# A two-block network on one core: layer 0's modulation dealt out in quarters of the contraction, the attention's scaling on two engines, and products that nobody reads in the last expert

## The chip, the core and the metric

The kernel runs on one core of a Trainium2 chip, which has its own TensorE (matrix products), VectorE (DVE), ScalarE (ACT), GpSimd (POOL), SyncE (SP, which here only issues transfers) and 16 DMA engines. The metric is the device time of one launch in microseconds (us). Lower is better.

## The reference

The model is two blocks on 256 tokens of width 1024. The first block is attention of two kinds and a mixture of experts; the second has two layers with adaptive modulation, of which each needs six vectors from a small conditioning vector:

```python
# first block
h = rms_norm(x, norm1_g);  proj = h @ w_in                      # 1024 -> 3072
oa = diff_attention(qa, ka, va, lam, ...)                       # 4 heads
oa = rms_norm(oa, subln_g) * (1 - lambda_init)
od = dilated_attention(qd, kd, vd, bias_b)                      # 8 heads
x = x + concat([oa, od]) @ w_out
x = x + expert_choice_ffn(rms_norm(x, norm2_g), ...)            # 16 experts take their 32 best tokens each
x = rms_norm(x, norm_f_g)
# second block, layer i of 2, on x and on a context of 256 tokens
mod   = silu(c)     @ ada_w[i] + ada_b[i]                       # 1024 -> 6144: shift, scale, gate, twice
mod_c = silu(c_ctx) @ ada_w[i] + ada_b[i]
h = x * (1 + sc1) + sh1;  y = mixer(h, ...)                     # MLA in layer 0, a windowed attention in layer 1
x = layer_norm(alpha * x + g1 * y, ln1_g[i], ln1_b[i])
x = layer_norm(alpha * x + g2 * mlp(x * (1 + sc2) + sh2), ln2_g[i], ln2_b[i])
```

All inputs are float32, and each weight is read once.

## The kernel before, in words

The program is one stream for each engine in a fixed order, written out by hand; a tile framework adds the waits. It has three parts.

**The front** (function `front`) computes the first block up to the router. After the first three projections, a loop over n runs 16 attention units (`units`: eight of the differential kind, then eight dilated) in a pipeline: unit n makes its scores (`sc`, L652), unit n-2 is turned (`dt`, L675) and multiplied with the values (`dpv`, L683 and L700). Between the two, a table (`fill`) says at which n one of the nine remaining projections runs (`prj`, 48 products of a split into high and low halves, L176 to L178), and a second one (`ADA_PULLS`) how many steps of layer 0's modulation are pulled. Such a step (`ada`) takes two tiles of 1 MB of `ada_w` (`adaw`, four buffers), multiplies them with the conditioning vectors into four strips of 32 partitions (`adap`, L476), copies the result to `adam`, and a step later adds the strips up by four narrow products (`adac`, L446), one step for each twelfth of the 6144 columns. At n = 15 the first 512 columns of the output `o` are scaled on DVE (L763); at the end `turn_o` transposes `o` (`trp`) for the output projection (`pyf`). Two of that projection's weights are converted on ACT and POOL at the n in `WOUT_AT`. The router then picks tokens with eight-at-a-time maxima on DVE (L845, L846), after a copy of the scores out of PSUM (L842).

**The experts** (`experts`) stream 16 experts' weights through a few buffers: gate and up (`wg`, products `egg` and `egu`, L970) and down (`wd`, `ey`, L1017). The context's layer 0 runs in between.

**The tail** (`tail`) adds the last expert's result (`esc`, L1849), normalises, and runs the second block on x. A list of steps (`filler`, pulled by `pull(fill)`) computes layer 1's modulation in the background of layer 0: the first half on TensorE, the second half on DVE (L497, L499, eight steps for a chunk, then `adac`). In layer 0's MLP another list, `rest`, applies the layer norm's gain and shift to x on POOL in eight steps (L1953).

SP issues nearly all loads in program order; a load waits for its buffer, and those behind it wait with it. POOL issues layer 1's `adaw` loads and some others in its own order.

Of the kernel before, what the change touches and what calls it, by code (L numbers as in the profile page):

```python
# [9 lines left out]
F32 = mybir.dt.float32  # L10
F32R = mybir.dt.float32r
AF = mybir.ActivationFunctionType
OP = mybir.AluOpType
# [6 lines left out]
NE = 16  # L20
CAP = 32
# [8 lines left out]
COLS = {}  # L30
# [71 lines left out]

ADA_PULLS = (0, 1, 0, 1, 0, 1, 0, 1, 0, 1, 0, 1, 1, 1, 1, 1, 1, 1)
MLA_PULLS = (3, 9, 13, 16)
PROJ_PULLS = (0, 0, 1, 0, 0, 0, 0)
ADA_VECTOR = 6
WOUT_AT = (15, 16)

UNITS = 11, 4, 8 * 11 + 11 * 4
CTX_FROM = 5 * 11
# [39 lines left out]
def pull(gen, n=1):  # L152
    for _ in range(n):
        next(gen, None)


def drain(gen):
    for _ in gen:
        pass


class Kernel:
# [24 lines left out]
    def bank(self, tag, shape, name):  # L187

        return self.psp.tile(shape, F32, name=name, tag=tag, bufs=2)

    def pair(self, name):

# [226 lines left out]
    def ada(self, layer, pool, nbuf, loader, q, q2, vector=12):  # L419
# [84 lines left out]
        yield 12  # L504
        gate_rows()

    def modulation(self, name, layer, kinds, who, g=None, b=None):

        nc = self.nc
        mod = (self.mod0, self.mod1)[layer]  # L510
        sh = mod[:, kinds[0] * 8:kinds[0] * 8 + 8, who]
        sc = mod[:, kinds[1] * 8:kinds[1] * 8 + 8, who]
        t = self.cm[name]

        def col(n):
            return self.cols[:, COLS[n][0]:COLS[n][0] + 8]
        if g is None:
            nc.vector.tensor_copy(t[:, 0], sc)
        else:
            nc.vector.tensor_mul(t[:, 0], sc, col(g))  # L520
        if b is None:
            nc.vector.tensor_copy(t[:, 1], sh)
        else:
            nc.vector.tensor_mul(t[:, 1], sc, col(b))
            nc.vector.tensor_add(t[:, 1], t[:, 1], sh)


    def front(self, es, right):
        tc, nc, a = self.tc, self.nc, self.a
        q = nc.gpsimd  # L530
# [22 lines left out]
        fe = ExitStack()  # L553
        fa = self.pool(fe, "fa")
        la = Loader({"a": 4})
        ag = self.ada(0, fa, 4, la, nc.sync, nc.gpsimd)
        next(ag)


# [21 lines left out]
        for k in range(0, 8, 2):  # L581
            p = trp[k // 2].rearrange("p (a b) -> p a b", a=2)
# [27 lines left out]
        n2, _ = COLS["norm2"]  # L610
# [30 lines left out]
        o = self.s8([128, 2, D], "o")  # L641
# [62 lines left out]
        g = proj(0)  # L704
# [18 lines left out]

        drain(g2)
        drain(proj(4))
        fill = {0: 1, 1: 3, 2: 5, 4: 6, 5: 8, 6: 10, 8: 7, 9: 9, 10: 11}
        units = [("diff", h, qt) for h in range(4) for qt in range(2)]
        units += [("dil", i, qt) for i in range(4) for qt in range(2)]
        or_ = f1.tile([128, 2, 4], F32, name="or_")
        oT = [fwl.tile([128, 8, 256], F32R, name="oT" + n, tag="hT" + n) for n in "hl"]  # L730

        def turn_o(k):
            p = self.transpose_to(o, k, 2, "d", "trp2")
            self.put(oT, (slice(None), slice(k, k + 2)), p, self.col("subln", 0) if k < 4 else None)
        pend = []
        for n in range(len(units) + 2):
            if n == WOUT_AT[0]:
                self.set_slots(own + [lambda nm: self.s8([128, 2048], nm, F32R) for i in range(2)])
            if n in WOUT_AT:
                self.convert(nc.gpsimd)  # L740
            if n < len(units):
                kind, i, qt = units[n]
                pend.append((kind, i, qt, (diff_a if kind == "diff" else dil_a)(i, qt)))
            done = pend.pop(0) if n >= 2 else None
            if done:
                kind, i, qt, e = done
                pt = turn(e, 1 if kind == "diff" else 2, "dt")
            g = proj(fill[n]) if n in fill else iter(())
            next(g, None)
            pull(ag, ADA_PULLS[n])  # L750
            if done:
                (diff_b if kind == "diff" else dil_b)(i, qt, pt)
                if qt == 1:
                    for h in ((i,) if kind == "diff" else (4 + 2 * i, 5 + 2 * i)):
                        if h + NB < 12:
                            load_bias(h + NB, q)
            drain(g)
            if n == 15:
                self.rstd(or_, ossq, 1.0 / 128, 1e-5)
                for t in range(2):  # L760
                    for h in range(4):
                        oo = o[:, t, h * 128:h * 128 + 128]
                        nc.vector.tensor_scalar(oo, oo, or_[:, t, h:h + 1], 1.0 - lam_init, op0=OP.mult, op1=OP.mult)  # L763
            if n >= 16:
                turn_o(2 * (n - 16))
        turn_o(4)
        turn_o(6)
        drain(ag)

# [48 lines left out]
        p = self.bank("d", [128, 2, NE], "rl")  # L818
# [19 lines left out]
        p = self.bank("d", [128, 256], "affT")  # L838
        for tt in range(2):
            nc.tensor.transpose(p[:NE, tt * 128:tt * 128 + 128], aff[:, tt], self.ident)  # L840
        wk = f1.tile([NE, 256], F32, name="wk", tag="hot")
        nc.vector.tensor_copy(wk, p[:NE])  # L842
        m8 = f1.tile([NE, 8], F32, name="m8")
        for _ in range(CAP // 8):
            nc.vector.max(m8, wk)  # L845
            nc.vector.match_replace(wk, m8, wk, -1.0)  # L846
        nc.vector.tensor_scalar(wk, wk, 0.0, None, op0=OP.is_lt)

        sw = f1.tile([NE, 256], F32, name="slotw", tag="addt")
# [77 lines left out]
    def experts(self, es, right, xs, oh, slots):  # L927
        tc, nc, a = self.tc, self.nc, self.a
# [27 lines left out]
        for e in range(NE):  # L956
# [3 lines left out]
            for k in range(8):  # L960
# [4 lines left out]
                for n in ("w_gate", "w_up"):  # L965
                    w = le.take((n, e, k))
# [44 lines left out]
            for n in range(11):  # L1011
                w = le.take(("d", e, n))
                for h in range(2):
                    for u in range(2):
                        r, q = (2 * (n // 2) + u, n % 2) if n < 10 else (10, u)
                        s = 2 * u + (h + n) % 2
                        nc.tensor.matmul(py[h][32 * s:32 * s + 32, :], hT[:, r, q], w[:, u, h * 512:h * 512 + 512],  # L1017
                                         start=n < 2, stop=n >= 9, skip_group_check=True)
                le.done(("d", e, n))
                if le.next == len(le.items) and self.lw.hold:  # L1020

                    self.lw.hold = None
                    self.lw.pump()
                context(UNITS[2] * e + 8 * UNITS[0] + UNITS[1] * (n + 1))
# [804 lines left out]
    def tail(self, es, sg, ye, py, jk):  # L1829
# [21 lines left out]
        with ExitStack() as e1:  # L1851
# [9 lines left out]
            def square(tt, h):  # L1861
                nc.scalar.activation(jk, x[:, tt, h * 512:h * 512 + 512], AF.Square, accum_out=st[:, tt, h:h + 1])
# [14 lines left out]
            hT = self.fm(8, True, "f", "hT")  # L1877
            self.convert(nc.gpsimd, nc.vector.tensor_copy)
            self.ahead = False
            drain(self.modulate_x(hT, x, "x0a", 0))  # L1880
            square(1, 1)
            norm(1)
            kT, v = self.s8([128, 8, 256], "kTx"), self.s8([128, 2, D], "vx")
# [8 lines left out]
            n = -1  # L1892
# [72 lines left out]
        with ExitStack() as e1:  # L1965
# [5 lines left out]
            for _ in self.mlp(0, 0, hT, True, acc, lambda *t: bt.done(*t), 1):  # L1971
                n += 1
                if n >= 4:
                    pull(fill)
                    pull(rest)
                if n == 16:
                    bt = Between(rows(0, 1, "ln2_g"), "x1a", "f")
            drain(fill)
            e0.close()
# [153 lines left out]
```

## Time and profile before

| | |
|---|---|
| time, median of 3 runs | 2386.43 us (2385.85 to 2392.71) |
| the profiled execution | 2387.11 us, its span 2385.3 us |
| TensorE busy | 85% of the span, granted clock 0.899 of full speed |
| VectorE, ScalarE, GpSimd busy | 34%, 23%, 11% |
| HBM read | 783.23 MB, 329 GB/s over the span |

The span begins with the first instruction and ends with the last; the 1.8 us between it and the execution's time lie around it. Full speed of TensorE's clock is 2.4 GHz, and 0.50 is 1.2 GHz. "Share" of the DMA engines is their mean busy share.

### The profile page before, as it was taken

To read this page: it belongs to the slowest core of one execution; us is meant where nothing else is said; L and a number is where in the kernel's file an instruction comes from. 1 tells how busy PE (TensorE), PEld (TensorE's weight loads), DVE (VectorE), ACT (ScalarE), POOL (GpSimd) and SP (SyncE) were. 2 spreads that over 40 slices of the span, in tenths; PEclk is the share of its full clock that TensorE was granted. 3 is DMA by queue.
4 is the path that set the end of the run, shared out by engine and by line. 5 is a ranking of instruction groups with operands and counts; after the bars stand their busy time and mean duration, and the time that the engine had idled before them with its cause. 6 is when DMAs were issued, how large, how long until landed. Compare 5 with 4: busy or idle time off the path is not lost.

```text
span 2385.3 us, 32056 instructions
## 1 busy us (share of the span) xinstructions
PE 2019.9 (85%) x13644; PEld 1250.3 (52%) x13644; DVE 811.1 (34%) x1484; ACT 551.8 (23%) x992; POOL 255.0 (11%) x274
## 2 busy tenths in 40 slices
PE   8998778887868777877888778777999999999998
PEld 7854223442214333333333333224888999987997
DVE  5653111121211111111111111304557765377655
ACT  5432010120000000000000000004444454276443
POOL 2121000000010000000000000003213012233101
PEclk9998888899968987888888788768998999999999
DMA  9788999999999999999999999998537864334652
GB/s 336 264 329 360 421 416 418 421 410 422 416 414 420 415 400 419 417 402 419 417 417 418 389 419 409 422 422 314 208 133 245 290 218 143 97 105 147 207 177 89
DMA packets 179223, 787.60 MB, mean 330 GB/s; under 512 B 13280, under 2 KB 73928, under 8 KB 125576
## 3 DMA queue, kind: packets, MB, share of 16 engines
q1 hardware_dynamic: 154648, 694.96, 73.8%
q0 software_dynamic: 24288, 89.54, 10.2%
q8 instruction: 107, 1.75, 0.3%
q10 hardware_dynamic: 144, 1.05, 0.1%
q14 instruction: 36, 0.29, 0.0%
HBM read 783.23 MB, written 2.27 MB: 329 GB/s over the span
## 4 chain that ended last, share of the span: by engine, by line
PE 46%; DMA 40%; DVE 3%; ACT 2%; issue 1%; DVEq 0%; ACTq 0%; SPq 0%
DMA wg<-in_w_up 26%; DMA wd<-in_w_down 10%; PE ey L1017 4%; PE egu L970 4%; DMA wg<-in_w_gate 4%; PE acc L176 3%; PE acc L178 3%; PE acc L177 3%; PE ph L176 3%; PE ph L177 3%; PE ph L178 3%; PE ph L174 2%; PE py L174 2%; PE egg L970 2%; PE nqkv L176 2%; PE nqkv L177 2%
## 5 line engine op out<-in xcount | busy, mean ns | idle before, releaser
L970 PE MATMUL egu<-wg,xeT 128*32 128x352 f32 x2048 | 217.3, 551 | 114.3 <-DMA wg<-in_w_up 114.2
L381 DVE TENSOR_TENSOR wl<-cwt,wh 128x1024 fp32r<-128x1024 f32 (+1 forms) x202 | 252.8, 1294 | 59.8 <-ACT wh L380 59.6
L1017 PE MATMUL ey<-wd,hT 128*32 128x512 f32 x1408 | 207.3, 703 | 71.4 <-DMA wd<-in_w_down 71.3
L970 PE MATMUL egg<-wg,xeT 128*32 128x352 f32 x2048 | 201.2, 515 | 62.1 <-DMA wg<-in_w_gate 62.1
L380 ACT CAST wh<-cwt 128x1024 fp32r<-128x1024 f32 (+2 forms) x218 | 214.5, 1033 | 95.0 <-issue 52.3
L970 PEld LDWEIGHTS egu<-wg,xeT 128*32 128x32 f32 x2048 | 65.1, 122 | 248.2 <-DMA wg<-in_w_up 172.3
L1498 ACT ACTIVATE hu<-ph 128x512 f32<-128x512 f32 x48 | 28.7, 597 | 554.2 <-PE ph L174 447.1
L970 PEld LDWEIGHTS egg<-wg,xeT 128*32 128x32 f32 x2048 | 57.8, 116 | 187.0 <-issue 93.4
L176 PE MATMUL ph<-hTxh,wh 128*128 128x256 f32 x512 | 147.0, 287 | 1.9 <-ACT hTxh L1116 1.9
L177 PE MATMUL ph<-hTxl,wh 128*128 128x256 f32 x512 | 146.7, 286 | 0.0
L178 PE MATMUL ph<-hTxh,wl 128*128 128x256 f32 x512 | 146.4, 286 | 0.0
L1017 PEld LDWEIGHTS ey<-wd,hT 128*32 128x32 f32 x1408 | 37.6, 118 | 204.7 <-DMA wd<-in_w_down 114.4
L1519 DVE TENSOR_TENSOR accc<-accc,py 128x512 f32<-128x512 f32 x60 | 41.3, 688 | 281.3 <-PE py L174 281.3
L174 PE MATMUL py<-cwt,hs 128*128 128x512 f32 x256 | 135.6, 677 | 0.0
L174 PE MATMUL ph<-hcT,cwt 128*128 128x256 f32 x512 | 134.6, 421 | 0.0
L174 PEld LDWEIGHTS ph<-hcT,cwt 128*128 128x128 f32 x512 | 106.1, 213 | 45.3 <-issue 29.6
L1501 DVE SCALAR_TENSOR_TENSOR hs<-ph,hu 128x512 f32<-128x512 f32 x16 | 11.1, 692 | 313.4 <-ACT hu L1498 313.4
L307 POOL DMA_DIRECT2D cwt<-in_w x32 | 25.7, 803 | 806.2 <-PE ph L174 340.6
L176 PEld LDWEIGHTS ph<-hTxh,wh 128*128 128x128 f32 x512 | 99.5, 194 | 2.9 <-ACT hTxh L1116 2.4
L177 PEld LDWEIGHTS ph<-hTxl,wh 128*128 128x128 f32 x512 | 99.3, 194 | 1.0 <-issue 0.5
L178 PEld LDWEIGHTS ph<-hTxh,wl 128*128 128x128 f32 x512 | 99.4, 194 | 0.0
L176 PE MATMUL acc<-wh,hsh 128*128 128x512 f32 (+1 forms) x256 | 98.6, 385 | 0.0
(546 smaller groups left out, 3502.8 us busy)
## 6 DMA issues: line engine op xcount, KB each, us to landing
wg<-in_w_gate SPq DMA_DIRECT2D x128, 1408.0 KB, 17.8
wg<-in_w_up SPq DMA_DIRECT2D x128, 1408.0 KB, 19.1
wd<-in_w_down SPq DMA_DIRECT2D x176, 1024.0 KB, 14.2
cwt<-in_w SPq DMA_DIRECT2D x64, 1024.0 KB, 5.3
cwt<-in_w POOLq DMA_DIRECT2D x32, 1024.0 KB, 14.0
adaw<-in_ada_w SPq DMA_DIRECT2D x24, 1024.0 KB, 8.6
adaw<-in_ada_w POOLq DMA_DIRECT2D x24, 1024.0 KB, 7.8
cwt<-in_w_in SPq DMA_DIRECT2D x12, 1024.0 KB, 10.2
```

The source lines that it names most:

```text
L174: t.matmul(out, L[0], R[0], start=start, stop=stop, **kw)
L176: t.matmul(out, L[0], R[0], start=start, stop=False, **kw)
L177: t.matmul(out, L[0], R[1], start=False, stop=False, **kw)
L178: t.matmul(out, L[1], R[0], start=False, stop=stop, **kw)
L307: q.dma_start(v, src)
L380: (high or nc.scalar.copy)(parts[0][:, s], t[:, s])
L381: (eng or self.low_eng).tensor_tensor(parts[1][:, s], t[:, s], parts[0][:, s].bitcast(F32), op=OP.subtract)
L970: nc.tensor.matmul(ps[n][h][32 * j:32 * j + 32, :352], xeT[:, k, e * CAP:(e + 1) * CAP], w[:, c0:c0 + 352], start=k == 0, stop=k == 7, ski ...
L1017: nc.tensor.matmul(py[h][32 * s:32 * s + 32, :], hT[:, r, q], w[:, u, h * 512:h * 512 + 512], start=n < 2, stop=n >= 9, skip_group_check=True)
L1498: nc.scalar.activation(u, p, AF.Relu)
L1501: nc.vector.scalar_tensor_tensor(h, p, 0.0, u, op0=OP.max, op1=OP.mult)
L1519: nc.vector.tensor_add(s, s, p)
```

## The change

Six edits are made together. (1) Layer 0's modulation is written anew (`ada_wide`): a step takes two of the eight row blocks of a third of the columns, in tiles of 128 rows x 2048 columns, so each row of a transfer is 8 KB long and no longer 2 KB. Four steps add their strips in `adam` on ACT (the first) and DVE (the others), and the strips of a whole third are then added up after four transposes. (2) `fill` and `ADA_PULLS` are spread anew over n, and `WOUT_AT` is one earlier. (3) The scaling of `o` is shared by ACT and DVE, with the constant factor folded into the row factors, and `turn_o` takes the unscaled columns first. (4) The router's first maximum reads PSUM, and the copy goes. (5) In the last expert two products of 128x128 by 128x256 follow each `wd` tile; nobody reads them (`busy`). Two more pairs stand around the tail's first transposes. (6) In layer 0's MLP `rest` is pulled at every third step, and the rows for the next norm are loaded at step 36 and not at 16.

```diff
-ADA_PULLS = (0, 1, 0, 1, 0, 1, 0, 1, 0, 1, 0, 1, 1, 1, 1, 1, 1, 1)
+ADA_PULLS = (0, 1, 0, 2, 0, 0, 2, 0, 0, 2, 0, 0, 1, 0, 1, 1, 1, 1)
-WOUT_AT = (15, 16)
+WOUT_AT = (14, 15)
...
+    def busy(self, n, tag):
+        p = self.bank(tag, [128, 512], "idle")
+        z = self.sc32.rearrange("p a b -> p (a b)")
+        for i in range(n):
+            self.nc.tensor.matmul(p[:, :256], z[:, :128], z, start=True, stop=True)
...
+    def ada_wide(self, layer, pool, nbuf, loader, q, q2):
...
+        for g in range(3):
+            m = pool.tile([128, 512], F32, name="adam", tag="adam", bufs=2)
+            for s in range(4):
+                p = self.bank(self.ada_tag, [128, 512], "adap")
+                for k in (2 * s, 2 * s + 1):
+                    t = loader.take(("a", g, k))
+                    for j in range(4):
+                        nc.tensor.matmul(p[32 * j:32 * j + 32, :], self.sc32[:, k, :], t[:, j * 512:j * 512 + 512],
+                                         start=k % 2 == 0, stop=k % 2 == 1, skip_group_check=True)
+                    loader.done(("a", g, k))
+                if s == 0:
+                    nc.scalar.copy(m, p)
+                    if last is not None:
+                        collect(*last)
+                else:
+                    nc.vector.tensor_add(m, m, p)
...
-        fill = {0: 1, 1: 3, 2: 5, 4: 6, 5: 8, 6: 10, 8: 7, 9: 9, 10: 11}
+        fill = {0: 1, 2: 3, 4: 5, 5: 6, 7: 8, 8: 10, 10: 7, 11: 9, 13: 11}
...
-                for t in range(2):
-                    for h in range(4):
+                nc.vector.tensor_scalar(or_, or_, 1.0 - lam_init, None, op0=OP.mult)
+                for h in range(4):
+                    for t in range(2):
                         oo = o[:, t, h * 128:h * 128 + 128]
-                        nc.vector.tensor_scalar(oo, oo, or_[:, t, h:h + 1], 1.0 - lam_init, op0=OP.mult, op1=OP.mult)
-            if n >= 16:
-                turn_o(2 * (n - 16))
-        turn_o(4)
+                        if t == 0:
+                            nc.scalar.activation(oo, oo, AF.Copy, scale=or_[:, t, h:h + 1])
+                        else:
+                            nc.vector.tensor_scalar(oo, oo, or_[:, t, h:h + 1], None, op0=OP.mult)
+            if n >= 15:
+                turn_o((4, 0, 2)[n - 15])
...
+                if e == NE - 1:
+                    self.busy(2, "d")
...
                     pull(fill)
-                    pull(rest)
-                if n == 16:
+                    if n % 3 == 0:
+                        pull(rest)
+                if n == 36:
```

How TensorE's order moves at unit 3 of the front: before, one modulation step (8 products `adap`) and its four narrow products stand between the turn of unit 1 (`dt`) and its values (`dpv`).

```order
L683 MATMUL dpv<-v,pt 128x128 x2
L652 MATMUL sc_685<-qk_220 128x256
L652 MATMUL sc_686<-qk_220 128x256
L675 MATMUL dt<-tabs_122,ae 128x128 x2
L476 MATMUL adap<-adaw,sc_89 32x512 x8
L446 MATMUL adac<-tabs_80,adam 128x2 x4
L683 MATMUL dpv<-v,pt 128x128 x2
```

The same place of the changed kernel, on TensorE (line numbers are its own):

```order
L755 MATMUL dpv<-v,pt 128x128 x2
L724 MATMUL sc_627<-qk_220 128x256
L724 MATMUL sc_628<-qk_220 128x256
L747 MATMUL dt<-tabs_122,ae 128x128 x2
L561 MATMUL adap<-adaw,sc_89 32x512 x16
L755 MATMUL dpv<-v,pt 128x128 x2
```

Two steps stand there now, and no `adac`; the unit still has no projection.

TensorE at the end of the front, from unit 16's modulation step to the last product before the output projection, before (`trp` are the transposes of `o`, `adar` turns a gate row):

```order
L476 MATMUL adap<-adaw,sc_89 32x512 x8
L446 MATMUL adac<-tabs_80,adam 128x2 x4
L700 MATMUL dpv_1665<-v,pt 128x64 x4
L239 MATMUL trp_1671<-tabs_80,o 128x128 x4
L675 MATMUL dt<-tabs_122,ae 128x128 x4
L476 MATMUL adap<-adaw,sc_89 32x512 x8
L446 MATMUL adac<-tabs_80,adam 128x2 x8
L461 MATMUL adar<-tabs_80,mod_85 16x128
L700 MATMUL dpv_1715<-v,pt 128x64 x4
L239 MATMUL trp_1721<-tabs_80,o 128x128 x4
L239 MATMUL trp_1728<-tabs_80,o 128x128 x4
L239 MATMUL trp_1735<-tabs_80,o 128x128 x4
```

And the same engine and place of the changed kernel:

```order
L561 MATMUL adap<-adaw,sc_89 32x512 x8
L772 MATMUL dpv_1613<-v,pt 128x64 x4
L246 MATMUL trp_1619<-tabs_80,o 128x128 x4
L747 MATMUL dt<-tabs_122,ae 128x128 x4
L561 MATMUL adap<-adaw,sc_89 32x512 x8
L534 MATMUL adac<-tabs_80,adam 128x128 x4
L772 MATMUL dpv_1652<-v,pt 128x64 x4
L246 MATMUL trp_1658<-tabs_80,o 128x128 x4
L246 MATMUL trp_1665<-tabs_80,o 128x128 x4
L547 MATMUL adar<-tabs_80,mod_85 16x128
```

Twelve narrow products became four transposes, one transpose group of `o` went to unit 15, and the gate row stands last.

POOL's order in layer 0's MLP, before (L1953 is the norm's gain and shift on x, L431 issues a load of layer 1's `adaw`, L466 writes a gate row):

```order
L1469 DMA row<-in_ln_b 128x1024
L1953 TENSOR_TENSOR xacc<-xacc,row 128x512
L466 DMA modrow_88<-adar 8x2x128
L1953 TENSOR_TENSOR xacc<-xacc,row 128x512 x3
L431 DMA adaw<-in_ada_w 128x4x512
L1953 TENSOR_TENSOR xacc<-xacc,row 128x512 x4
L431 DMA adaw<-in_ada_w 128x4x512 x2
```

POOL at the same place of the changed kernel:

```order
L473 DMA modrow_88<-adar 8x2x128
L1546 DMA row<-in_ln_b 128x1024
L2032 TENSOR_TENSOR xacc<-xacc,row 128x512
L438 DMA adaw<-in_ada_w 128x4x512
L2032 TENSOR_TENSOR xacc<-xacc,row 128x512
L438 DMA adaw<-in_ada_w 128x4x512
L2032 TENSOR_TENSOR xacc<-xacc,row 128x512 x2
L438 DMA adaw<-in_ada_w 128x4x512
L2032 TENSOR_TENSOR xacc<-xacc,row 128x512
```

The runs of three and four additions became ones and twos with a load between each.

## Rows read from the trace of the kernel before

**Rows 1.** The page: granted clock and transfer rate in 40 slices of the span.

```profile
PEclk9998888899968987888888788768998999999999
...
GB/s 336 264 329 360 421 416 418 421 410 422 416 414 420 415 400 419 417 402 419 417 417 418 389 419 409 422 422 314 208 133 245 290 218 143 97 105 147 207 177 89
```

**Rows 2.** Busy time by window of the front: PE, PEld, DVE, ACT, POOL, clock, DMA.

```profile
120.00:140.00 20.00, 19.41 (x157) 11.60 (x156) 10.49 (x47) 6.74 (x21) 0.94 (x2) 1.00 1.03 371
...
220.00:240.00 20.00, 18.34 (x215) 8.95 (x214) 4.86 (x10) 2.90 (x4) 0.00 (x0) 0.91 1.00 419
```

**Rows 3.** Timeline, unit 14 on TensorE: start, duration, operation, [idle before].

```profile
136.55 1.92 PE L476 MATMUL adap<-adaw,sc 128*32 128x512 f32 x16
138.41 1.05 PE L446 MATMUL adac<-tabs,adam 128*128 128x2 f32 x8
139.32 1.08 PE L700 MATMUL dpv<-v,pt 128*128 128x64 f32 x8
...
141.55 1.92 PE L476 MATMUL adap<-adaw,sc 128*32 128x512 f32 x16
```

**Rows 4.** Timeline of units 15 to 17 and the start of the output projection.

```profile
141.73 4.66 POOL L381 TENSOR_TENSOR wl<-cwt,wh 128x1024 fp32r<-128x1024 f32 x2 [6.42 <-ACT wh L380]
141.88 2.25 DVE L657 TENSOR_SCALAR amx<-amx 128x2 f32<-128x2 f32 x1
...
147.56 1.08 PE L700 MATMUL dpv<-v,pt 128*128 128x64 f32 x8 [3.10 <-DVE mod L448]
...
149.11 5.26 DVE L763 TENSOR_SCALAR o<-o,or__424 128x128 f32<-128x128 f32 x8
149.20 3.37 PE L476 MATMUL adap<-adaw,sc 128*32 128x512 f32 x16
...
154.33 0.61 PE L239 MATMUL trp<-tabs,o 128*128 128x128 f32 x4
...
163.98 0.48 PE L176 MATMUL pyf<-wh,oTh 128*128 128x512 f32 x1
```

**Rows 5.** SP's waits from 20 to 160 us: total, times, longest.

```profile
SPq L307 <- DVE wl L381: 58.8, 10, 8.1
```

**Rows 6.** The chain that ended last, at the router.

```profile
193.74 0.42 DVE wk L842
```

**Rows 7.** Timeline of the last expert and the tail's start.

```profile
1605.76 3.00 PE L1017 MATMUL ey<-wd,hT 128*32 128x512 f32 x24
...
1616.49 1.94 PE L1017 MATMUL ey<-wd,hT 128*32 128x512 f32 x8 [0.57 <-DMA wd<-in_w_down]
...
1626.57 1.84 PE L1017 MATMUL ey<-wd,hT 128*32 128x512 f32 x8 [1.51 <-DMA wd<-in_w_down]
...
1629.06 5.92 PE L1849 MATMUL esc<-sgye 128*128 128x512 f32 x8 [0.65 <-ACT sgye L1842]
1630.26 1.35 ACT L380 CAST wh<-cwt 128x640 fp32r<-128x640 f32 x2 [1.26 <-DMA cwt<-in_dkv]
```

**Rows 8.** Timeline: like products at full clock, earlier in the experts.

```profile
265.84 3.89 PE L1033 MATMUL esc<-ye,sg 128*128 128x512 f32 x8 [0.68 <-ACT ye L1028]
...
910.38 3.72 PE L174 MATMUL ph<-hcT,cwt 128*128 128x256 f32 x16
```

**Rows 9.** Timeline of POOL, DVE and PE in layer 0's MLP.

```profile
1812.16 3.36 DVE L499 SCALAR_TENSOR_TENSOR adam<-adaw,sc,adam 128x512 f32<-128x512 f32 x1
...
1818.82 0.74 DVE L499 SCALAR_TENSOR_TENSOR adam<-adaw,sc,adam 128x512 f32<-128x512 f32 x1
...
1820.67 6.96 POOL L1953 TENSOR_TENSOR xacc<-xacc,row 128x512 f32<-128x512 f32 x4
...
1833.25 1.84 PE L446 MATMUL adac<-one,adam 128*128 128x1 f32 x8 [3.83 <-DVE adam L499]
```

**Rows 10.** Windows of that place, columns as in Rows 2.

```profile
1832.00:1836.00 4.00, 2.75 (x11) 2.59 (x12) 3.27 (x7) 2.27 (x3) 0.79 (x1) 0.50 0.89 286
1836.00:1840.00 4.00, 4.00 (x14) 3.23 (x13) 3.36 (x4) 0.24 (x1) 0.00 (x0) 0.71 1.02 345
```

More of the change, by code (lines that the diff above doesn't have):

```diff
@@ L505, in ada, with fn, collect, gate_row @@
         gate_rows()
+    def ada_wide(self, layer, pool, nbuf, loader, q, q2):
+        nc = self.nc
+        w = self.a["ada_w"][layer]
+        for g in range(3):
+            for k in range(8):
+                def fn(src=w[k * 128:(k + 1) * 128, g * 2048:(g + 1) * 2048]):
+                    t = pool.tile([128, 2048], F32, name="adaw", tag="adaw", bufs=nbuf)
+                    q.dma_start(t, src)
+                    return t
+                loader.add(("a", g, k), "a", fn)
+        yield
+        mod = (self.mod0, self.mod1)[layer]
+        o, _ = COLS["adab"]
+        bcol = self.cols[:, o + 48 * layer:o + 48 * layer + 48]
+        def collect(g, m):
+            p = self.bank(self.ada_tag, [128, 4, 128], "adac")
+            for i in range(4):
+                nc.tensor.transpose(p[:, i], m[:, i * 128:i * 128 + 128], self.ident)
+            pv = p.rearrange("p i (s r) -> p r s i", s=4)
+            for half in range(2):
+                c0 = 16 * g + 8 * half
+                for i in range(2):
+                    nc.vector.scalar_tensor_tensor(
+                        mod[:, c0:c0 + 8, i].rearrange("p (s i) -> p s i", s=2), pv[:, i, 2 * half:2 * half + 2],
+                        1.0 if 2 * g + half in (1, 4) else 0.0,
+                        bcol[:, c0:c0 + 8].rearrange("p (s i) -> p s i", s=2), op0=OP.add, op1=OP.add)
+        def gate_row(n):
+            c0 = (16, 40)[n]
+            p = self.bank("d", [128, 128], "adar")
+            nc.tensor.transpose(p[:16, :], mod[:, c0:c0 + 8].rearrange("p a b -> p (a b)"), self.ident)
+            r = pool.tile([16, 128], F32, name="adar", tag="adar", bufs=1)
+            nc.vector.tensor_copy(r, p[:16, :])
+            d = self.modrow[layer]
+            q2.dma_start(bass.AP(tensor=d.tensor, offset=d.offset + n * 1024, ap=[[128, 8], [2048, 2], [1, 128]]), r)
+        last = None
+        for g in range(3):
+            m = pool.tile([128, 512], F32, name="adam", tag="adam", bufs=2)
[13 more added lines that the diff above has]
+                    nc.vector.tensor_add(m, m, p)
+                if s == 1 and g == 2:
+                    gate_row(0)
+                if g < 2 or s < 3:
+                    yield g
+            last = (g, m)
+        collect(*last)
+        yield 3
+        gate_row(1)
@@ L555, in front @@
         la = Loader({"a": 4})
-        ag = self.ada(0, fa, 4, la, nc.sync, nc.gpsimd)
+        ag = self.ada_wide(0, fa, 4, la, nc.sync, nc.gpsimd)
         next(ag)
@@ L841, in front @@
         wk = f1.tile([NE, 256], F32, name="wk", tag="hot")
-        nc.vector.tensor_copy(wk, p[:NE])
         m8 = f1.tile([NE, 8], F32, name="m8")
-        for _ in range(CAP // 8):
-            nc.vector.max(m8, wk)
-            nc.vector.match_replace(wk, m8, wk, -1.0)
+        for i in range(CAP // 8):
+            src = wk if i else p[:NE]
+            nc.vector.max(m8, src)
+            nc.vector.match_replace(wk, m8, src, -1.0)
         nc.vector.tensor_scalar(wk, wk, 0.0, None, op0=OP.is_lt)
@@ L1879, in tail @@
             self.ahead = False
+            self.busy(2, "c")
             drain(self.modulate_x(hT, x, "x0a", 0))
+            self.busy(2, "c")
             square(1, 1)
```

## The prediction

> **What bounds the kernel now.** I read the page first: transfer rate and clock in slices [rows 1]. From the fifth slice to the 27th (240 to 1610 us) the rate stands near 418 GB/s. That is the experts' stream, and transfers bound it; nothing in it is changed but its last expert. Before it and behind it the rate is lower and the clock mostly at 9 of 10, so there TensorE or a chain of waits sets the time. What is saved ahead of the stream moves the whole stream forward, since the transfers start again only when TensorE frees the first expert tiles; what is saved behind it moves the end. So each part of the change is priced in its own stage, and the prices add.
>
> In the front I took windows and the timeline. From 120 to 140 us TensorE is busy 19.41 of 20 us at full clock [rows 2]. A late unit has 5.00 us from one modulation step to the next (136.55 to 141.55), and rows fill it without a gap [rows 3]. But the DMA share is 1.03 in the same window, at 371 GB/s, so the loads of `adaw` are close behind. Units 15 to 17 are different: DVE stands behind POOL, TensorE idles 3.10 us, and the step after it takes 3.37 us, not 1.92 [rows 4].
>
> In the last expert TensorE waits for `wd`, and its clock falls and rises: the same eight records take 1.94 us at half speed, and the last tile's take 1.84 [rows 7]. In layer 0's MLP TensorE is busy all the time but for one wait of 3.83 us for DVE [rows 9], with half clock behind it [rows 10].
>
> **The change part by part.**
>
> *Modulation in the front.* The products `adap` stay 96 in number and size, 1.92 us a step. A step's `adac` begins 0.91 us ahead of what follows (138.41 to 139.32) [rows 3]. Twelve of them go, 10.9 us. Three groups of four transposes come, 0.61 us each by `trp` [rows 4], 1.8 us. Net -9.1 us of an engine that hardly idles. The additions into `adam` take the place of copies of the same tile on DVE and ACT, so I put them at nothing; TensorE's next work (a turn, values, scores) covers them. At the third's end they have no cover: there `adac` follows its own last addition.
>
> *Units 14 to 17.* Before, the idle time and the half clock cost 3.10 + (3.37 - 1.92) = 4.55 us [rows 4]. Their cause: POOL's conversion of 4.66 us holds up a 2-element operation on DVE for 2.25 us, and behind it queue DVE's row scaling and the copy of the turned scores, for which `dpv` waits. The change does not remove this. With `WOUT_AT` one earlier both conversions now meet units that make scores, 14 and 15. What gets better is the copy: without `adam` in the alternation all the dilated units' turned scores are copied on ACT, so they no longer stand behind DVE's row scaling. I charge two stalls of 1.75 us (bounds: two of 3.10, and none), against 4.55: 2 x 1.75 - 4.55 = -1.0, between +1.7 and -4.6. The scaling of `o`, 5.26 us on DVE alone, is shared by two engines and lies under unit 16's turn, step and values, so I put it at nothing; without that cover TensorE would wait for what is left of it, 2.6 us. One group of transposes moves out of the end, -0.6 us by its 0.61.
>
> *Loads of the front.* The new table asks for four tiles at once at n = 3, 6 and 9, and all but two of those at n = 3 are issued a unit or more ahead. SP's order puts them behind weight loads that wait for conversions, 8.1 us at most, 5.9 us on average [rows 5]. I charge 1.3 us, mostly at n = 3, between 0 and 5.
>
> Front: -9.1 - 1.0 - 0.6 + 1.3 = -9.4 us, between -14 and -3.
>
> At the late units the step of two tiles (2.1 MB) costs 2.1/371 = 5.65 us of transfer at the measured rate, and TensorE would now want one every 4.4 to 5. Rows 11 KB long, the experts', move at 419 GB/s with share 1.00 [rows 2], which would be 5.0 us; the new rows of 8 KB are nearer to those. Four tiles wait in the buffers at n = 14, since n = 13 has a projection and no step, so I see no stall there. The Trainium skill ("DMA: Bandwidth & Descriptors", Specifications) says that transfers reach line rate from 512 bytes on. By that rule 2 KB and 8 KB rows are alike, and the late steps would be bound by their loads; the two windows, 371 against 419 GB/s, speak against it, though other loads are mixed into both.
>
> *Router.* The copy of 0.42 us goes [rows 6]; the first maximum and replacement read PSUM in its place. -0.4 us, or -0.2 if these get longer.
>
> *Last expert and tail's start.* Two products cost about 0.93 us at full clock (sixteen records, eight products, in 3.72) [rows 8]. A tile's own take about 1.0 at full clock (half of 1.94), and tiles come every 2.52 us (four from 1616.49 to 1626.57) [rows 7]. So the pairs lie in the wait for `wd`, and TensorE is busy three quarters of the time. If the clock then stays full, the last tile takes about 1.0 in place of 1.84, and `esc` 3.89 [rows 8] in place of 5.92 [rows 7]; the last pair delays `esc` by 0.3 us. That would be 2.5 us, but ACT stands in the way: it waits for a weight transfer until 1630.26 and casts it for 1.35 us [rows 7] before its first square. The chain then runs over that cast and ACT's two squares and no longer over `esc`, so I take a little over half: -1.4, between -3 and +0.5. The pairs around the transposes lie in TensorE's waits there, and the clock was already full, so nothing.
>
> *Layer 0's MLP.* POOL's additions hold DVE: an operation of 0.74 us took 3.36, and four additions in a row took 6.96 us [rows 9]. Seven of the eight stood in two runs with one load between, the last ending at 1827.63, and DVE was still behind when TensorE reached `adac` at 1829.42. That operation lost 2.62 us under a run of three, some 0.9 for each addition, so seven cost DVE about 6 us and the three that now fall into this stretch 2.6. The wait of 3.83 should go, or nearly. With it goes half clock: (1 - 0.50) x 2.75 + (1 - 0.71) x 4.00 = 2.5 us [rows 10]. 3.83 + 2.5 = 6.3. The other additions now fall into later chunks, where DVE has more room; I give back 0.9 for a short wait at a later `adac`. -5.4, between -6.3 and -1.5. The later row loads (step 36) are wanted only at the MLP's end, 25 steps on, so nothing.
>
> **Sum.** -9.4 - 0.4 - 1.4 - 5.4 = -16.6 us. The profiled execution took 2387.11 us, 1.8 more than its span of 2385.3, and the change touches nothing that lies around the span: 2387.1 - 16.6 = 2370.5. The median of the three runs is 0.7 lower, so the same sum from it gives 2369.8. I say **2370 us**, a ratio of 0.993.
>
> **The rivals.**
>
> *A. The port wait is only moved.* POOL's eight additions still meet a busy DVE; if the delay gathers at the next `adac` or two, the 5.4 us come back: 2375. The Trainium skill ("SBUF — State Buffer", Who interferes with whom) says that the port pair of DVE and GpSimd is an exclusive lock and the loser blocks for the whole instruction. Rows 9 agree (3.36 against 0.74). By that rule the total of blocked time would be the same however it is spread. For it: DVE is 3.27 to 3.36 us busy in each 4 us there [rows 10]. Against: the wait came only behind a cluster.
>
> *B. The front is bound by loads or stalls, not by TensorE.* If late steps go at 5.65 us, or both stalls are full ones, the front gives 4 us and not 9.4: 2375. For it: share 1.03 [rows 2]. Against: TensorE was busy 97% in that window.
>
> *A and B together:* 2380.5.
>
> *C. No stall at all.* All bounds at their good end, -14, -0.4, -3, -6.3: 2363.
>
> *D. Slower: the products bind the last expert.* If the clock stays at half there, a tile costs 1.94 for its own products and 1.86 for the two others, 3.8 us against 2.5 of transfer. Eleven tiles are then 41.8 us and not the 22.65 from 1605.76 to 1628.41 [rows 7], +19.1. With the other gains, -15.2, the kernel ends at 2390. It decides as soon as a tile's products exceed 2.5 us. Against it: with TensorE busy throughout, the clock came back (0.50, then 0.71) [rows 10].
>
> *E. Slower: the double steps outrun SP.* If each of the three waits the longest 8.1 us [rows 5], +24, less 1.3 counted: 2393. It decides from 6.0 us each on, where it has eaten the other 17.9.
>
> **How the numbers follow.** The sum as worked out 0.47, A 0.12, B 0.16, C 0.13, A and B 0.07, D 0.03, E 0.02. 0.3% of the time is 7.2 us, about what a measurement of this kernel can tell from no change. Faster by more: the first four, 0.88. Within 0.3%: A and B together, and D and E near their prices, 0.09. Slower by more: D or E beyond their prices, 0.03. The range goes from C's 2362 to 2381, the case of A and B, and leaves out some 0.07 at the slow end.
>
> **What would show it.** The output projection (`pyf`) should begin near 154.6 us, not 163.98, and the first `egg` as much earlier. Units 14 and 15 should show a TensorE idle time of 1 to 2 us each. The last `wd` tile's products should take about 1.06 us, with a window clock near 1.0 from 1600 on, and `esc` about 3.9. In layer 0's MLP no wait for `adam` over 1 us and no slice of half clock. The prediction is wrong if `adap` waits for DMA in the front, if the stream's end does not move with `pyf`, or if the wait of 3.83 us turns up elsewhere.

## The result, and the profile after

The changed kernel takes **2368.28 us** (median of 4 runs, 2367.44 to 2369.50) against 2388.33 us (2385.85 to 2392.71) for the kernel before in the same series, a ratio of 0.9914 with a 95% interval of [0.9897, 0.9932]. The forecast was 2370. The profiled execution after took 2369.50 us, with a span of 2367.4 us; TensorE is busy 85% of it as before, and its mean granted clock is 0.908 and no longer 0.899.

The gain in the two profiles, read off as the shift of the same instruction between them:

| up to the start of | before | after | gain so far |
|---|---|---|---|
| `pyf`, the output projection | 163.98 | 157.46 | 6.5 |
| `egg`, the first expert | 205.06 | 198.19 | 6.9 |
| the last expert's `eht` | 1602.87 | 1592.66 | 10.2 |
| `pdkv`, the tail's first projection | 1638.94 | 1626.29 | 12.7 |
| `ph`, layer 0's MLP | 1791.01 | 1778.30 | 12.7 |
| the span's end | 2385.3 | 2367.4 | 17.9 |

The timeline of TensorE at the end of the front, after (start, duration, operation, idle time before it and what ended it). It answers to [rows 3, 4], and its first row to the term for the loads:

```profile
58.32 1.06 PE L561 MATMUL adap<-adaw,sc 128*32 128x512 f32 x8 [1.25 <-DMA adaw<-in_ada_w]
...
132.12 0.66 PE L534 MATMUL adac<-tabs,adam 128*128 128x128 f32 x4
133.97 1.10 PE L772 MATMUL dpv<-v,pt 128*128 128x64 f32 x8 [1.19 <-ACT pt L183]
...
136.94 2.79 PE L561 MATMUL adap<-adaw,sc 128*32 128x512 f32 x16
...
142.06 1.92 PE L772 MATMUL dpv<-v,pt 128*128 128x64 f32 x8 [2.12 <-ACT pt L183]
...
145.61 3.56 PE L561 MATMUL adap<-adaw,sc 128*32 128x512 f32 x16
...
153.92 0.66 PE L534 MATMUL adac<-tabs,adam 128*128 128x128 f32 x4 [0.81 <-DVE adam L569]
...
157.46 0.48 PE L176 MATMUL pyf<-wh,oTh 128*128 128x512 f32 x1
```

The stalls of units 14 and 15 are there, 1.19 and 2.12 us. Behind them `adap` takes 2.79 and 3.56 us where 1.92 is its time at full clock. What makes `pt` late is seen on the other engines, in the timelines of POOL, DVE and ACT of the same kernel:

```profile
135.69 4.68 POOL L388 TENSOR_TENSOR wl<-cwt,wh 128x1024 fp32r<-128x1024 f32 x2
136.80 3.61 DVE L729 TENSOR_SCALAR amx<-amx 128x2 f32<-128x2 f32 x1
140.44 0.51 ACT L731 ACTIVATE ae<-ae,amx 128x256 f32<-128x256 f32 x1 [4.15 <-DVE amx L729]
...
141.44 0.56 ACT L183 COPY pt<-dt 128x512 f32<-128x512 f32 x1
```

POOL's conversion holds a 2-element operation on DVE for 3.61 us, ACT's exponentials wait 4.15 us for that, the copy `pt` stands behind them in ACT's queue, and `dpv` waits for `pt`. Once unit 14's `dpv` has started, this chain and not TensorE sets when unit 15's can: 8.09 us later in after and in experiments 1 and 4. In experiment 7 it is 8.10, and there unit 15's `adap` ran at full clock; TensorE only waited longer.

The last expert and the tail's start in the timeline of after (against [rows 7]; `idle` is the tile of the products that nobody reads):

```profile
1614.37 1.06 PE L1092 MATMUL ey<-wd,hT 128*32 128x512 f32 x8
1615.36 1.13 PE L196 MATMUL idle<-sc 128*128 128x256 f32 x4
1616.42 1.07 PE L1092 MATMUL ey<-wd,hT 128*32 128x512 f32 x8
...
1618.36 1.35 ACT L387 CAST wh<-cwt 128x640 fp32r<-128x640 f32 x2 [0.26 <-DMA cwt<-in_dkv]
1618.38 3.60 PE L1926 MATMUL esc<-sgye 128*128 128x512 f32 x8
```

From the second tile on a tile's own products take 1.06 us, TensorE has no gap, and `esc` takes 3.60 us where it took 5.92. So TensorE is busy all the time here and not three quarters of it: a tile costs it 2.06 us. The first tiles lie ready in their buffers, and so the eleven took 22.65 us before as well, again 2.06 each, though the later ones came every 2.52. The last tile lands at 1616.29, and its products start at 1616.42: two products for a tile are just as many as fit.

Layer 0's MLP in windows of after (columns as in [rows 2], against [rows 10]):

```profile
1790.00:1810.00 20.00, 20.00 (x126) 17.85 (x125) 15.28 (x20) 8.94 (x11) 4.59 (x5) 1.00 0.84 280
1810.00:1830.00 20.00, 20.00 (x139) 18.65 (x138) 14.53 (x18) 7.99 (x10) 5.41 (x5) 1.00 0.81 270
```

POOL's timeline there:

```profile
1816.09 2.64 POOL L2032 TENSOR_TENSOR xacc<-xacc,row 128x512 f32<-128x512 f32 x2
```

TensorE is busy 20 us of 20, at full clock. POOL's additions come one or two at a time, 1.3 us each; four in a row took 6.96 [rows 9]. None of DVE's operations on `adam` takes more than 0.75 us.

### The profile page after: what moved, and what is told of

Read it like the earlier page. It is cut to its first block, busy times and chain, and to the rows that moved or that the text cites. A ratio compares the mean times of both kernels' runs of the same rounds, so it can differ in the third digit from the quotient of the medians.

```text
span 2367.4 us, 31973 instructions
## 1 busy us (share of the span) xinstructions
PE 2009.7 (85%) x13612; PEld 1244.8 (53%) x13612; DVE 801.4 (34%) x1471; ACT 552.3 (23%) x993; POOL 253.6 (11%) x274
## 3 DMA queue, kind: packets, MB, share of 16 engines
q8 instruction: 107, 1.75, 0.3%
## 4 chain that ended last, share of the span: by engine, by line
PE 46%; DMA 39%; DVE 3%; ACT 2%; issue 1%; DVEq 0%; ACTq 0%
DMA wg<-in_w_up 30%; DMA wd<-in_w_down 10%; PE egu L1045 4%; PE ey L1092 4%; PE acc L176 3%; PE acc L178 3%; PE acc L177 3%; PE ph L177 3%; PE ph L176 3%; PE ph L178 3%; PE py L174 2%; PE egg L1045 2%; PE ph L174 2%; PE nqkv L176 2%; PE nqkv L177 2%; PE nqkv L178 2%
## 5 line engine op out<-in xcount | busy, mean ns | idle before, releaser
L1092 PE MATMUL ey<-wd,hT 128*32 128x512 f32 x1408 | 197.6, 668 | 71.0 <-DMA wd<-in_w_down 70.5
```

## The experiments

The first three undo or do one part each, on top of the kernel before; the others are edits of the changed kernel. The kernel before ran in each series and had a median of 2388.85 us with the first four, 2388.45 with the next four and 2390.16 with the last two.

**1. The front alone.** The kernel before with edits 1 to 3 of the change.

> The kernel before with the edits of the front alone: the modulation in quarters, both tables, WOUT_AT one earlier, the shared scaling and the new order of the turns of o. The whole change brought pyf forward by 6.5 us and shortened the stretch from the first eht to the last by 3.4 us (1363.6 to 1360.2). Theory: the front gives its 6.5 us one to one and the 3.4 us of the stream are chance between executions, so the time is 6 to 7 us under the kernel before, with pyf near 157.5, and the stretch between the ehts is again anywhere between 1360 and 1364. Rival: the earlier or rearranged loads of the front make the stream itself shorter, then 9 to 10 us under the kernel before and a stretch near 1360. Rival of the other kind: what the front gains is taken back at the stream's start, then under 4 us.

Measured: 2377.50 us, ratio 0.9949 [0.9933, 0.9966], 11.4 us faster than before. In its profile `pyf` starts at 154.92, and the stretch between the first and the last expert's `eht` is 1362.09 us long. The 11.4 us (by the interval 8.1 to 16.0) are above the ranges of theory and rival, but the stream is hardly shorter, as the theory had it: it is the front, the same as in the changed kernel, that is 2.5 us shorter in this profile.

**2. The MLP alone.**

```diff
                     pull(fill)
-                    pull(rest)
-                if n == 16:
+                    if n % 3 == 0:
+                        pull(rest)
+                if n == 36:
```

> The kernel before with only the last edit: rest at every third step of layer 0's MLP, the row loads at step 36. Theory: the wait of 3.83 us for adam and the half clock behind it go, 5.2 to 5.4 us faster, no wait for adam over 1 us in the MLP. Rival: without the other edits the gathering of POOL's additions only moves to a later adac, then 1 us or less.

Measured: 2381.17 us, ratio 0.9960 [0.9945, 0.9975], 7.7 us faster, and by the interval at least 6.0, so a little more than expected. There is no wait for `adam` in the MLP. From the first `ph` to the span's end it takes 587.2 us; the three kernels without this edit (before, and experiments 1 and 3) take 594.3 each. Its front is that of the kernel before, and still `pyf` starts at 166.09 and not at 163.98.

**3. The products alone.** The kernel before with `busy` in the last expert and around the tail's first transposes.

> The kernel before with only the products nobody reads, in the last expert and around the tail's first transposes. Theory: they hold the clock, esc takes 3.6 to 3.9 us and not 5.92, and the time from the last expert's eht to the first pdkv falls from 36.07 us to about 33.6: 2.4 us faster in all. Rival: that gain came from the earlier weight transfers of the whole change and not from the products, then 0 to 1 us, with esc still short. Second rival: the products delay the last tile's own, 1 us slower.

Measured: 2385.79 us, ratio 0.9986 [0.9977, 0.9996], 3.1 us faster. In its timeline the end of the last expert reads:

```profile
1626.77 1.06 PE L1024 MATMUL ey<-wd,hT 128*32 128x512 f32 x8
1627.76 1.13 PE L196 MATMUL idle<-sc 128*128 128x256 f32 x4
1628.73 3.60 PE L1858 MATMUL esc<-sgye 128*128 128x512 f32 x8
```

From the last `eht` to `pdkv` it takes 33.77 us, as in the changed kernel (33.63); without the products it was 36.07 (before), 36.47 (experiment 1) and 36.78 (experiment 2). So the products, and nothing else in the change, give this gain. It lies ahead of the tail's transposes: from the first `mtx` to `pdkv` it is 2.69 us before and 2.70 here, so nothing is seen of the two pairs around them. Again `pyf` starts late, at 166.40.

The three parts add up to 11.35 + 7.68 + 3.06 = 22.1 us against 20.05 of the whole change, no more apart than the intervals allow.

**4. Four products for a tile.** `self.busy(4, "d")` in place of `self.busy(2, "d")` in the last expert.

> The changed kernel with four products for each wd tile of the last expert in place of two. By the row of after a pair takes 1.13 us and a tile's own products 1.06, so a tile would cost 3.3 us against 2.5 of transfer, and TensorE binds: eleven tiles end 11 x 3.3 = 36.5 us after 1595.6 and not 22.8, so 13 to 14 us slower than the changed kernel, near 2382. That is the point from which the prediction's rival D decides. If instead the transfers bound all along and the products still found room, it would stay within 2 us of 2368.

Measured: a single run of 2383.11 us, 13.6 above the changed kernel's profiled execution (2369.50). Of these, 3.3 us were there before the last expert (its `eht` at 1595.99). The rows of its timeline:

```profile
1605.31 1.06 PE L1092 MATMUL ey<-wd,hT 128*32 128x512 f32 x8
1606.30 1.99 PE L196 MATMUL idle<-sc 128*128 128x256 f32 x8
1608.23 1.06 PE L1092 MATMUL ey<-wd,hT 128*32 128x512 f32 x8
```

A tile now costs 2.92 us and no longer 2.06, and `esc` comes 32.6 us behind the first `ey` where it came 22.8 behind it: 9.8 us slower. TensorE binds, as rival D had it, but by the number of products and not by a half clock, which D assumed: the rows run at full clock. I had put the tile at 3.3 since I doubled a row of 1.13 that overlaps its neighbours.

**5. The turn ahead of the scores** in units 14 and 15, so that `pt` stands ahead of the exponentials on ACT.

```diff
-            if n < len(units):
-                kind, i, qt = units[n]
-                pend.append((kind, i, qt, (diff_a if kind == "diff" else dil_a)(i, qt)))
+            def make():
+                if n < len(units):
+                    kind, i, qt = units[n]
+                    pend.append((kind, i, qt, (diff_a if kind == "diff" else dil_a)(i, qt)))
+            if n not in WOUT_AT:
+                make()
...
                 pt = turn(e, 1 if kind == "diff" else 2, "dt")
+            if n in WOUT_AT:
+                make()
```

> The changed kernel, but in units 14 and 15 the turn of the older unit (dt and its copy pt) stands ahead of the new unit's scores. In the profile of after dpv waits there 1.19 and 2.12 us for pt, which stands on ACT behind exponentials that wait for a 2-element operation of DVE, which is held by POOL's conversion (1.73 and 3.61 us). Theory: with pt ahead of the exponentials both waits go (3.3 us), and so does the half clock behind them, of which the first front kernel shows that 2.5 us are chance: 3 to 6 us faster than the changed kernel, 2362 to 2365. Rival: the scaling of o and the last turns wait for the same late DVE operations, so the wait only moves from dpv to trp or pyf: 0 to 1 us.

Measured: 2367.98 us (2367.12 to 2371.02), ratio to before 0.9913 [0.9898, 0.9927], as the change. The rival was right:

```profile
139.24 1.01 PE L772 MATMUL dpv<-v,pt 128*128 128x64 f32 x8
146.01 1.11 PE L246 MATMUL trp<-tabs,o 128*128 128x128 f32 x4 [5.76 <-DVE adar L549]
```

Both waits at `dpv` are gone, and TensorE waits 5.76 us at `trp`, whose bank DVE must free first; POOL holds DVE as before.

**6. Holding the clock, in the bank of `dt`.**

```diff
             pull(ag, ADA_PULLS[n])
+            if n in WOUT_AT:
+                self.busy((2, 6)[n - 14], "d")
```

> The changed kernel with two and six products that nobody reads ahead of dpv in units 14 and 15, in TensorE's waits there. Theory: the waits stay (they are set by POOL, DVE and ACT), but the clock stays full behind them: dpv 1.92, trp 1.06, dt 1.06 and adap 3.56 us of unit 15 and 16 fall to 1.08, 0.61, 0.66 and 1.92, together 3.3 us faster than the changed kernel, near 2365. Rival: six products last longer than the wait, 0 to 1 us.

Measured: 2368.74 us (2368.03 to 2373.50), ratio 0.9918 [0.9902, 0.9934]. The six products waited for `pt` themselves, and then stood in its way:

```profile
141.57 4.30 PE L196 MATMUL idle<-sc 128*128 128x256 f32 x12 [3.71 <-ACT pt L183]
145.70 1.00 PE L772 MATMUL dpv<-v,pt 128*128 128x64 f32 x8
...
147.68 1.92 PE L561 MATMUL adap<-adaw,sc 128*32 128x512 f32 x16
```

As a remedy this failed, but it prices the clock: from this `dpv` to `pyf` it is 12.31 us at full clock, and 15.40 in after. The products themselves cost more than that: 4.13 us from their start to this `dpv`.

**7. Rows of 2 KB in the new layout.**

```diff
-                def fn(src=w[k * 128:(k + 1) * 128, g * 2048:(g + 1) * 2048]):
+                def fn(src=w[k * 128:(k + 1) * 128].rearrange("p (j g c) -> p j g c", j=4, g=3)[:, :, g]):
```

> The changed kernel, but each tile of layer 0's modulation takes its 2048 columns as four pieces of 512, so each row of a transfer is again 2 KB long and no longer 8 KB (the modulation's columns come in another order, so the values of layer 0's modulation are others; all durations are as before). Theory of the prediction: 2 KB rows move slower (371 GB/s in the kernel before, against 419 of 11 KB rows), the front's loads fall behind, adap waits for DMA in more units than n = 3, and the kernel is 2 to 5 us slower than the changed one. Rival, by the Trainium skill (DMA: Bandwidth & Descriptors, Specifications), which sees no loss from 512 bytes on: the same rate in the windows of the front and the same time within 1 us.

Measured: 2369.10 us (2366.31 to 2372.49), ratio 0.9916 [0.9899, 0.9932]. No loss in the time can be measured. The front as one window, first after, then this kernel:

```profile
24.00:128.00 104.00, 101.39 (x819) 82.89 (x818) 64.70 (x169) 52.67 (x120) 11.49 (x16) 1.00 0.93 339
```

```profile
24.00:128.00 104.00, 100.93 (x812) 82.11 (x812) 62.29 (x167) 51.76 (x119) 11.21 (x16) 1.00 0.96 333
```

At 333 GB/s the DMA share is 0.96, at 339 it was 0.93 (and 0.92 at 338 and 337 in experiments 1 and 4): the queues work some 5% longer for a byte. TensorE, busy 101 of 104 us, hardly waits for it: 1.7 us at n = 3, against 1.25, 0.4 and 1.4 in after and experiments 1 and 4, and nothing in units 14 to 17.

**8. No POOL in units 14 and 15:** `self.convert(nc.vector)` in place of `self.convert(nc.gpsimd)`.

> The changed kernel, but in units 14 and 15 the low halves of the two converted weights are made by DVE and not by POOL. Theory (POOL's two operations of 4.67 us hold DVE's small operations, 1.73 and 3.61 us in place of about 0.1): no operation of DVE is held in these units; DVE gets 2 x 1.1 us more of its own in each, ahead of the scores' maxima, and must wait for ACT's cast. The wait of 2.12 us at unit 15 goes or falls under 1 us, the one of 1.19 at unit 14 stays: 1 to 4 us faster than the changed kernel. Rival: what holds pt is ACT's own queue (two casts of 2.0 us), then both waits stay as they are, and the time too.

Measured: 2366.79 us (2364.06 to 2371.49), ratio 0.9902 [0.9885, 0.9918], which is not to be told from the change. DVE's 2-element operation takes 0.30 us in both units. TensorE's timeline:

```profile
134.75 1.97 PE L772 MATMUL dpv<-v,pt 128*128 128x64 f32 x8 [2.13 <-ACT pt L183]
...
142.09 1.00 PE L772 MATMUL dpv<-v,pt 128*128 128x64 f32 x8
...
149.77 1.06 PE L561 MATMUL adap<-adaw,sc 128*32 128x512 f32 x8 [1.33 <-DMA adaw<-in_ada_w]
152.06 1.93 PE L561 MATMUL adap<-adaw,sc 128*32 128x512 f32 x8 [1.22 <-DMA adaw<-in_ada_w]
```

Unit 15's wait is gone, unit 14's has grown (DVE's own conversion waits for ACT's cast, ahead of the scores' maxima), and 2.55 us went to the loads of unit 17.

**9. Holding the clock, in another bank:** experiment 6 with `"c"` in place of `"d"`.

> As the sixth kernel (two and six products that nobody reads, in TensorE's waits of units 14 and 15), but into a PSUM bank that is free by then: there the six stood in the bank of dt, waited themselves for pt and added 4.30 us behind the wait, and yet pyf came at 158.01 against 157.46. Theory: what follows dpv then runs at full clock (12.3 us from dpv of unit 15 to pyf, as there, not 15.4 as in after, less the 4.3 of the products counted inside neither), pyf near 154.5, about 3 us faster than the changed kernel, near 2365. Rival: the clock that is held comes back later as half clock at pyf or the router (the 185 to 200 us stretch), then 0 to 1 us.

Measured: 2368.23 us (2365.31 to 2369.67), ratio 0.9912 [0.9895, 0.9930]. Inconclusive. The granted clock is 1.00 in every window from 120 to 185 us, and yet `pyf` comes at 158.91. Three waits for `adaw` cost 4.0 us in this execution, one of them behind the held stretch, and the products of unit 14 waited 1.69 us for the bank of the former `adap`.

**10. Experiments 5 and 8 together.**

> The fifth and the eighth kernel together: dt and pt ahead of the scores in units 14 and 15, and the low halves of the two weights made by DVE. Turn first alone moved the wait to trp (5.76 us, behind the copy of adar that DVE could not make while POOL held it); DVE alone moved it to unit 14 (2.13 us for pt) and to the loads of unit 17 (1.33 and 1.22 us). Theory: both causes go, POOL's lock and ACT's queue, no wait over 1 us is left at dpv or trp in units 14 to 16, and what binds next are the loads of unit 17, whose buffers come free only with unit 15's step: pyf between 152 and 155, 2 to 5 us faster than the changed kernel, 2363 to 2366. Rival: the loads take back all of it, as in the eighth kernel, then the time is within 1 us of 2368.

Measured: 2368.90 us (2365.91 to 2369.41), ratio 0.9914 [0.9894, 0.9933]. The front is shorter, but by less than the sum of its waits:

```profile
137.66 1.10 PE L772 MATMUL dpv<-v,pt 128*128 128x64 f32 x8 [0.24 <-ACT pt L183]
142.40 1.12 PE L246 MATMUL trp<-tabs,o 128*128 128x128 f32 x4 [3.64 <-DVE adar L549]
...
155.13 0.48 PE L176 MATMUL pyf<-wh,oTh 128*128 128x512 f32 x1
```

From unit 13's `dpv` to `pyf` it takes 26.6 us, and 29.3 in after, but 27.7 in experiment 1, with the same front as after. The wait at `trp` is still there, at 3.64 us: DVE's own conversion, 2.36 us, now stands ahead of the scores' maxima in its queue. What is won, 1.0 to 2.7 us, does not show in the median. No version beats the changed kernel by more than the measurement can tell.

## Why the prediction was right

**Front, forecast -9.4.** The two profiles alone give -6.5 at `pyf`. But the front of the kernel before ran in three profiles, with `pyf` at 163.98, 166.09 and 166.40, and the new front, unaltered, in three as well: 157.46, 154.92 and 158.01. The means, 165.49 and 156.80, are 8.7 us apart. At the last expert's `eht` the same profiles are 9.3 us apart, and experiment 1 gave 11.4 in the time. So the term was about right, and the profile on which the sum rests caught a short front.

What makes fronts with the same instructions differ can be read in part. In experiment 2, 1.7 us of the 2.1 come from half clock in the first projections. The window (columns as in [rows 2]), first before, then experiment 2:

```profile
18.00:22.00 4.00, 3.83 (x27) 3.37 (x27) 3.01 (x5) 2.44 (x4) 3.71 (x5) 0.87 1.01 294
```

```profile
18.00:22.00 4.00, 3.32 (x15) 3.07 (x15) 3.01 (x5) 2.35 (x3) 3.71 (x5) 0.50 0.97 284
```

In experiment 3, 1.6 us of the 2.4 come from half clock in one `dt` and one `adap` (1.11 and 2.98 us for 0.66 and 1.92). They stand behind a wait of 0.48 us; the kernel before has the same wait, and full clock behind it. Between after and experiment 1 it is a wait for `adaw`, 0.9 us, and the half clock behind unit 15, 1.7.

The parts of the term: up to unit 14's `dpv`, eight of the twelve groups of `adac` had run before, and two of the three groups of transposes have run after. By the prediction's prices that is 8 x 0.91 - 2 x 0.61 = 6.1 us. The two profiles give 7.8 (139.32 against 133.97, less the waits of 1.19 and 1.25), so the modulation's part was right or a little small. Two stalls charged at 1.75 each were 1.19 and 2.12. POOL's hold on DVE was named rightly, and `pt` no longer stood behind DVE's row scaling; it stood behind ACT's exponentials, which the prediction had not seen. The loads, charged at 1.3, cost 1.25 in after, 0.4 in experiment 1 and nothing ahead of unit 14 in experiments 6, 8 and 10, but 3.3 in experiment 5 and 3.1 in 9. Ahead of unit 14 these have the same instructions, so the spread is one between executions.

The step that failed is the half clock: I charged stalls "of 1.75" and nothing behind them. Between the two stalls it costs nothing, since the chain over ACT sets the pace there. Behind the second it does: from unit 15's `dpv` to `pyf` it took 15.40, 13.72 and 15.38 us in the three profiles against 12.31 at full clock, another 1.4 to 3.1. That the sum comes out even so is luck in part.

The weighing of the rows, "the new rows of 8 KB are nearer to those", was not shown: experiment 7 finds no difference in the time between 2 KB and 8 KB. The Trainium skill ("DMA: Bandwidth & Descriptors", Specifications) puts line rate at 512 bytes and more, and the time agrees; the extra share per byte, 5%, that section doesn't show. But the fear tied to the rule did not come true either: no `adap` of units 14 to 17 waited for its load, in the changed kernel or with rows of 2 KB. Only where a stall was taken away or filled (experiments 8 and 9) did unit 17 wait for `adaw`.

**Router, -0.4.** The copy of 0.41 us is gone, the first maximum takes 0.42 us from PSUM as from SBUF, and from `affT` to `slT` (the transposes ahead of the maxima and behind them) it is 6.64 us in place of 6.99. But experiment 1, which keeps the copy, has 6.63. Behind the maxima stands an operation of DVE on `wk`, here in after and then in experiment 1:

```profile
191.07 0.93 DVE L922 TENSOR_SCALAR wk<-wk 16x256 f32<-16x256 f32 x1
```

```profile
188.99 0.50 DVE L915 TENSOR_SCALAR wk<-wk 16x256 f32<-16x256 f32 x1
```

It ends 5.40 us behind `affT`'s start in both, 0.15 us behind POOL's subtraction `xn2l`, which began at 0.60; before, these were 5.75, 0.15 and 0.95. So the number came out, but the copy's time went into a longer wait for POOL; why POOL began 0.35 us earlier in the kernels with the new front is open.

**The stream, 0.** In the two profiles it is 3.4 us shorter. I take it for chance: over twelve kernels the stretch between the ehts is 1358.9 to 1363.6 us, and experiments 2 and 3, which have the front of before, show 1359.5 and 1359.2.

**Last expert and tail's start, -1.4.** The mechanism was right and the size too small. Without the products the stretch is 36.07 to 36.78 us, with two of them 33.62 to 34.37 (eight profiles): about -2.6, the full price that I had worked out before halving it. The step that failed is "ACT stands in the way". That step took the transfer of `dkv` to land as late as before. But the cast now starts with `esc` (1618.36 against 1618.38) and not 1.2 us behind it as in [rows 7], since the transfer lands 25.4 to 25.6 us behind the last `eht` in after and experiments 3, 4 and 6, and 27.1 to 27.9 in the three profiles without the products. So ACT's first square at 1620.17 waits for the sum that follows `esc`, and not for the cast. Why the transfer comes earlier, though it is issued later (13.1 us behind the `eht` in after, 10.4 before), is not shown.

**Layer 0's MLP, -5.4.** From the first `ph` to the end: 594.3 us in the three profiles without the edit, 587.2 to 589.9 in nine with it, mean 588.6: -5.6. There is no wait for `adam` over 1 us, and no half clock in the windows shown. This settles rival A: the blocked time did not stay the same. Two of DVE's operations on `adam` were held before, 3.36 and 1.78 us for 0.75, and in the nine profiles with the edit none was. POOL's additions fall to 1.3 us each; before, they took up to 2.2. The lock itself is there: DVE's 2-element operation takes 1.73 and 3.61 us under POOL's conversion, and 0.30 without it (experiment 8). This agrees with the Trainium skill ("SBUF — State Buffer", Who interferes with whom). That the total of blocked time would be the same however it is spread was my own inference, and it was wrong here.

**The rivals.** B (loads or full stalls) did not come true in the time of the changed kernel. C came true in part: last expert and MLP were at or near their good ends, but the front was not. D's condition was set at products over 2.5 us a tile; TensorE binds from 2.06 on, since the first tiles are ready. Experiment 4, at 2.92, cost 9.8 us. D's half clock was not seen: from 1600 us on the granted clock is 1.00 in the last expert. E was not seen: the largest wait for `adaw` in any front was 2.0 us. Of the signs of being wrong, one did appear, `adap` waiting for DMA in the front, 1.25 us at n = 3. It was stated too broadly, since the sum itself charged 1.3 for it.

The end sum, -8.7 - 0.4 - 2.6 - 5.6 = -17.3, lies within the interval of the time (the ratio's bounds, taken of 2388.33: -16.2 to -24.6); the remaining 2.7 to the difference of the medians, 20.05, is not assigned.

## What to carry to other kernels

One profile is one draw: if unchanged stages differ by 2 to 4 us between executions, read a stage's term from the same stretch in several kernels, not from the two profiles of the change alone. A stall on TensorE can have a second price behind it, its half clock, where TensorE sets the pace; ahead of another wait it costs nothing. Products that nobody reads fill a stall only where their PSUM bank is free at that moment, and even there (experiment 9) no gain in the time could be measured. And taking away one wait at a place where POOL, DVE, ACT and the loads are all nearly late only names the next one: experiments 5, 8 and 9 each removed what they were aimed at, 10 a part of it, and all left the time as it was.

## What the runs showed of the hardware that was not expected

A pair of products for each tile, 1.13 us in 2.06, kept the granted clock at 1.00 in every window of the last expert from 1600 us on. A wait of 1.19 us in unit 14 of the changed front was followed by half clock in all three profiles of that front (`adap` of unit 15 took 2.79, 3.23 and 2.70 us against 1.92), but in experiment 7 a wait of 1.20 us at the same place was not (1.92). Yet unit 15's `dpv` started 8.09 or 8.10 us behind unit 14's in all four. And the same stream of transfers, with the same instructions, differs in length by up to 4.7 us in 1360.
